# Rotary rows of a latent-attention encoder step: low parts taken before the halves are exchanged, rotations ended later in program order, key halves added on the vector engine

## The chip, the core and the metric

The kernel runs on one core of one Trainium2 chip. A core has a matrix engine (TensorE, PE in the profile; its weight loads are listed as PEld), a vector engine (VectorE, DVE), a scalar engine (ScalarE, ACT), a general engine (GpSimd, POOL) and an engine that here only issues DMAs (SyncE, SP; its queue is SPq in the profile). Each engine works through its own instructions in order and waits at one until what it needs is there. The metric is the device time of one execution in microseconds, as the median of several runs.

## What is computed

The program is one inference step of a one-layer encoder over 512 prompt frames and 32 frames of a running stream, 544 rows together: a layer norm, an input projection, eight heads of a gated linear recurrence, eight heads of latent attention, an output projection, and a gated feed-forward part. The change concerns the latent attention alone:

```python
q = (rms_norm(cq, q_a_g) @ w_q_b).reshape(B, T, MLA_HEADS, QK_NOPE + QK_ROPE)   # 128 + 64 per head
q_nope = q[..., :QK_NOPE]
q_rope = apply_rope(q[..., QK_NOPE:], cos[:, None, :], sin[:, None, :])
lat_new = rms_norm(ckv, kv_a_g)
kr_new = apply_rope(kr, cos, sin)
...
kv = (lat @ w_kv_b).reshape(B, past_len + T, MLA_HEADS, QK_NOPE + V_HEAD)
s = (jnp.einsum('bqhd,bkhd->bhqk', qn, k_nope)
     + jnp.einsum('bqhd,bkd->bhqk', qr, k_rope)).astype(jnp.float32) * scale

def apply_rope(x, cos, sin):
    x1, x2 = jnp.split(x, 2, axis=-1)
    return jnp.concatenate([x1 * cos - x2 * sin, x1 * sin + x2 * cos], axis=-1)
```

All results are float32.

## The kernel before

**Number format.** Most operands of matmuls are kept in the type `fp32r` (`R` in the code) in two parts, a high part (x rounded, by ACT) and a low part (x minus the high part, by DVE), and a product is the sum of high x high, high x low and low x high. `split_w` and `piece` do this for weights (L106 on ACT, L107 on DVE), `split_act` for activations (L176, L177), `mm3` issues the three products (L118).

**Layout.** Activations lie with features on the 128 partitions and the 544 rows along the free axis. Eight attention heads are worked on as four pairs. `proj_pair(pr)` computes for a pair the rotary query rows (`t == 2`, the 64 rotary features of both heads on 128 partitions), the plain query rows of each head (`t` 0 and 1), the plain keys `kn` of each head (L542, emptied by L546) and the values `vt` (L555, emptied by L558). `attend(pr)` computes scores (L585 plain, L587 rotary, mask at L588), the softmax, the transposes (L602, L603) and the value products (L616), in blocks of 128 queries; `scores` with `b == 4` is the running stream.

**Rotation.** `rope` exchanges the two halves of 32 features by four DMAs into `sw`, multiplies x by the cosines on POOL (in place, so after the DMAs have read x), `sw` by the sines on DVE, and adds the two on DVE into its targets. A rotary query tile `qr` of one head holds its 64 rounded rows on one half of the partitions and the low parts of these rows on the other, while the rotary key stands twice, `krs` rows 0 to 63 and again 64 to 127; one matmul thus takes both parts. To get the low part on the other half, `proj_pair` sends the rotated rows (`xr`) to the other partitions by two DMAs (`xo`, L525), rounds them there again on ACT (`xh`, L527) and subtracts on DVE (L530).

**Key rotation.** `kr_proj` multiplies by weights that hold their high parts in 64 columns and their low parts in the next 64, so that the two parts of the key come out on two halves of the partitions (L476). A matmul with a matrix `fold` of two identities adds them and puts the sum on both halves (L486). The outcome is rotated into `krs` and split into `krh` and `krl`.

**Memory.** The projections write PSUM tiles `main`, of which there are two; a third can only start once the first has been copied out (`hold`, on ACT). Temporaries of 128x544 come from the pool `t` with 7 buffers.

**Order.** The functions are generators. `weave` issues a few steps of a first list (projections) and then a step of a second (norms, attention). This gives the program order, and a scheduler of the language decides from it the order on every engine; within an engine nothing overtakes. All loads of weights and all DMAs of the rotation are issued by SP, in one queue.

Of the kernel before, what the change touches and what calls it, by code (L numbers as in the profile page):

```python
# [7 lines left out]
F32 = mybir.dt.float32  # L8
# [7 lines left out]
P = 128  # L16
D = 2048
KD = D // P
TP = 512
# [40 lines left out]
def tile_encoder_step(ctx, tc, xp, xs, w_in, w_in4, w_kr, w_q_b, w_kv_b, w_out, w_up, w_gate, w_down, w_down2,  # L60
# [31 lines left out]
    def main_tile():  # L92
        return psm.tile([P, 1024], F32, name="main", tag="main")
# [270 lines left out]
    with tc.tile_pool(name="mp", bufs=1) as mp, tc.tile_pool(name="psa", bufs=4, space=PSUM) as psa:  # L364
# [10 lines left out]
        krh = mp.tile([P, TP], R, name="krh")  # L375
# [10 lines left out]
        def tt():  # L386
            return mp.tile([P, T], F32, name="t", tag="t", bufs=7)
# [31 lines left out]
        def rope(x, dst_parts):  # L419
            sw = tt()  # L420
            for b in range(2):
                o = b * 64
                dma(sw[o:o + 32, :], x[o + 32:o + 64, :])
                dma(sw[o + 32:o + 64, :], x[o:o + 32, :])
            G.tensor_tensor(out=x, in0=x, in1=cos, op=ALU.mult)
            V.tensor_tensor(out=sw, in0=sw, in1=sin, op=ALU.mult)
            for dst, r, a, b in dst_parts:
                V.tensor_tensor(out=dst, in0=x[r, a:b], in1=sw[r, a:b], op=ALU.add)
# [37 lines left out]
        def kr_proj():  # L466
# [13 lines left out]
            fold, kp = tt()[:, :P], tt()  # L480
            for b in range(2):
                V.tensor_tensor(out=fold[:, 64 * b:64 * b + 64], in0=ident[:, :64], in1=ident[:, 64:], op=ALU.add)
            A.activation(kp, hold(kt), AF.Copy)
            kt = main_tile()
            for ps, j in both(kt):
                PE.matmul(ps, fold, kp[:, H_[j]], start=True, stop=True)  # L486
            kx = tt()
            A.activation(kx, hold(kt), AF.Copy)
            rope(kx, [(krs[:, :TP], slice(0, P), 0, TP), (krs[:, TP + PAST:], slice(0, P), TP, T)])
            dma(kr_d[:, :TP], krs[0:64, :TP])  # L490
            dma(kr_d[:, TP:], krs[0:64, TP + PAST:])
            krl = c["krl"] = hp.tile([P, T], R, name="krl", tag="hproj")[:, :TP]
            A.activation(krh, krs[:, :TP], AF.Copy)
            V.tensor_tensor(out=krl, in0=krs[:, :TP], in1=krh.bitcast(F32), op=ALU.subtract)
# [4 lines left out]
        def proj_pair(pr):  # L499
# [7 lines left out]
            qs = []  # L507
            for t in (2, 0, 1):
# [8 lines left out]
                if t == 2:  # L517
                    qr = ropes[pr % 2]
                    halves = list(enumerate((slice(0, 64), slice(64, P))))
                    xr, xo = tt(), tt()  # L520
                    rope(x, [(xr[:, :TP], slice(0, P), 0, TP)]
                         + [(qlast[pr % 2][r, 2, j * TS:(j + 1) * TS], r, TP, T) for j, r in halves])
                    xh = mp.tile([P, T], R, name="xh", tag="t", bufs=7)
                    for j, r in halves:
                        dma(xo[halves[1 - j][1], :TP], xr[r, :TP])  # L525
                        A.activation(qr[j][r], xr[r, :TP], AF.Copy)
                    A.activation(xh[:, :TP], xo[:, :TP], AF.Copy)  # L527
                    for j, r in halves:
                        o = halves[1 - j][1]
                        V.tensor_tensor(out=qr[j][o], in0=xo[o, :TP], in1=xh[o, :TP].bitcast(F32), op=ALU.subtract)  # L530
                    qs.append(qr)
                else:
                    G.tensor_copy(qlast[pr % 2][:, t, t * TS:(t + 1) * TS], x[:, TP:])
                    qs.append(x)
# [25 lines left out]
            pairs[pr] = qs[1:], qs[0], kn, vt  # L560
# [12 lines left out]
        def attend(pr):  # L573
# [3 lines left out]
            def scores(b, j):  # L577
# [8 lines left out]
                for i, k in enumerate((krh, c["krl"])):  # L586
                    PE.matmul(sc[:, :nk], qr[j][:, q0:q0 + P], k[:, :nk], start=False, stop=i == 1)  # L587
# [47 lines left out]
        weave([head_qf(0)], [ckv_norm()], 0.5)  # L635
# [1661 lines left out]
```

## Time and profile before

| | us |
|---|---|
| median of 3 runs | 2372.44 |
| lowest, highest | 2371.78, 2375.01 |
| the profiled execution | 2373.59 |
| its span, from the first to the last instruction | 2371.8 |
| TensorE busy in the span | 2320.4 |
| VectorE busy | 1801.2 |
| ScalarE busy | 1066.5 |
| GpSimd busy | 120.9 |
| mean granted clock of TensorE | 0.993 |

The span is what the views of the profile cover; the execution's own time has 1.8 us around it. A busy time is the sum of an engine's instructions; a matmul overlaps the next one, so the step from start to start, not the duration, says what one costs in a row. In a row of the timeline stand the start, the duration, engine, line, operation, the tile written and the tiles read, the shape, and how many equal instructions were merged; in brackets the idle time ahead and what ended it. The granted clock is the share of full speed at which TensorE ran.

The attention part with its projections lies between 70 and 310 us of the span. The input projection of the queries' norm comes before; the recurrence, the output projection and the feed-forward part come after.

### The profile page before, as it was taken

The numbers are of one execution on the slowest core, as the hardware profiler recorded it, in microseconds if no ns is written. First come the engines' busy times: TensorE is split into PE (matmuls) and PEld (weight loads), VectorE is DVE, ScalarE is ACT, GpSimd is POOL, SyncE is SP. The second block draws the span as 40 slices with busy tenths as digits, with TensorE's granted clock in tenths as the row PEclk, the third lists the DMA queues.
The fourth block names the chain that finished last, engine by engine and source line by source line (L and its number), as shares of the span: only waits on it lengthen the run. The fifth ranks groups of instructions, "written<-read, shape, count | busy, mean of one in ns | idle before, by whom it ended". The sixth has DMA issues, their size and how long they took to land.

```text
span 2371.8 us, 44419 instructions
## 1 busy us (share of the span) xinstructions
PE 2320.4 (98%) x18434; PEld 2303.8 (97%) x18434; DVE 1801.2 (76%) x2492; ACT 1066.5 (45%) x1659; POOL 120.9 (5%) x159
## 2 busy tenths in 40 slices
PE   7989999999999999999999999999999999999997
PEld 6989999999999999999999999999999999999997
DVE  7436668777786448989888888888777888888566
ACT  5335434433443226655555555555444433333334
POOL 1000000000001211000000000000000100000013
PEclk9999999999999999999999999999999999999998
DMA  7222263222235235544535435354343973643322
GB/s 243 90 87 71 75 205 99 87 85 86 91 133 199 90 107 198 164 165 144 194 113 165 149 121 192 105 178 135 112 131 118 363 295 115 238 139 96 108 73 76
DMA packets 128969, 334.25 MB, mean 141 GB/s; under 512 B 12032, under 2 KB 60928, under 8 KB 124160
## 3 DMA queue, kind: packets, MB, share of 16 engines
q1 hardware_dynamic: 121936, 285.73, 36.4%
q0 software_dynamic: 6832, 45.68, 4.9%
q8 instruction: 145, 2.38, 0.4%
q14 instruction: 56, 0.46, 0.1%
HBM read 272.78 MB, written 56.15 MB: 139 GB/s over the span
## 4 chain that ended last, share of the span: by engine, by line
PE 91%; DVE 4%; issue 2%; ACT 2%; DMA 1%; POOL 0%; SPq 0%; ACTq 0%; DVEq 0%; POOLq 0%
PE main L1248 21%; PE acc L1248 16%; PE main L118 14%; PE main L788 11%; PE main L1279 8%; PE acc L1279 6%; PE acc L118 6%; PE s L853 2%; PE main L555 1%; PE main L542 1%; PE at L616 1%; DVE wl L1194 1%; PE at L585 1%; PE sw L885 0%; PE sw L917 0%
## 5 line engine op out<-in xcount | busy, mean ns | idle before, releaser
L1193 ACT ACTIVATE wh<-raw 128x1024 fp32r<-128x1024 f32 x347 | 367.4, 1060 | 433.1 <-DVE raw L1186 132.7
L1194 DVE TENSOR_TENSOR wl<-raw,wh 128x1024 fp32r<-128x1024 f32 x347 | 424.3, 1223 | 131.2 <-ACT wh L1193 130.0
L1248 PE MATMUL main<-op,wh 128*128 128x272 f32 x1408 | 265.5, 287 | 0.0
L1248 PE MATMUL acc<-ops,wh 128*128 128x272 f32 x1344 | 254.2, 287 | 0.0
L1248 PE MATMUL main<-ops,wh 128*128 128x272 f32 x1344 | 254.2, 287 | 0.0
L1248 PEld LDWEIGHTS main<-op,wh 128*128 128x128 f32 x1408 | 221.0, 188 | 0.0
L1248 PEld LDWEIGHTS acc<-ops,wh 128*128 128x128 f32 x1344 | 211.0, 188 | 0.0
L1248 PEld LDWEIGHTS main<-ops,wh 128*128 128x128 f32 x1344 | 211.0, 188 | 0.0
L1248 PE MATMUL main<-op,wl 128*128 128x272 f32 x704 | 203.0, 288 | 0.3 <-DVE wl L1194 0.3
L1248 PE MATMUL acc<-ops,wl 128*128 128x272 f32 x672 | 193.7, 288 | 0.0
L1248 PE MATMUL main<-ops,wl 128*128 128x272 f32 x672 | 193.7, 288 | 0.0
L118 PE MATMUL main<-aH,wh 128*128 128x272 f32 (+2 forms) x736 | 176.8, 296 | 0.4 <-ACT wh L280 0.4
L118 PE MATMUL main<-aH,wl 128*128 128x272 f32 (+2 forms) x736 | 172.0, 290 | 3.0 <-DVE wl L281 3.0
L118 PE MATMUL main<-aL,wh 128*128 128x272 f32 (+2 forms) x736 | 171.9, 290 | 0.4 <-DVE aL L269 0.4
L1248 PE MATMUL acc<-op,wh 128*128 128x272 f32 x832 | 159.1, 289 | 3.5 <-DVE eg L1475 3.5
L107 DVE TENSOR_TENSOR wl<-raw,wh 128x1024 fp32r<-128x1024 f32 (+2 forms) x72 | 80.2, 1115 | 90.0 <-ACT wh L106 86.1
L1186 DVE TENSOR_TENSOR raw<-raw,raw 128x1024 f32<-128x1024 f32 x114 | 139.4, 1223 | 2.7
L732 ACT ACTIVATE wh<-raw 128x1024 fp32r<-128x1024 f32 x84 | 88.7, 1056 | 111.7 <-DVE raw L727 102.8
L1248 PEld LDWEIGHTS acc<-op,wh 128*128 128x128 f32 x832 | 131.7, 190 | 3.7 <-issue 3.7
L1248 PEld LDWEIGHTS main<-op,wl 128*128 128x128 f32 x704 | 132.3, 188 | 0.5 <-DVE wl L1194 0.5
L1194 DVE TENSOR_TENSOR wl<-rawl,wh 128x1024 fp32r<-128x1024 f32 x86 | 105.1, 1222 | 31.1 <-ACT wh L1193 31.1
L1193 ACT ACTIVATE wh<-rawl 128x1024 fp32r<-128x1024 f32 x86 | 91.0, 1059 | 82.3 <-DVE rawl L1186 42.4
(439 smaller groups left out, 6087.3 us busy)
## 6 DMA issues: line engine op xcount, KB each, us to landing
raw<-in_w_in SPq DMA_DIRECT2D x76, 512.0 KB, 3.6
raw<-in_w_up SPq DMA_DIRECT2D x72, 512.0 KB, 4.2
raw<-in_w_gate SPq DMA_DIRECT2D x72, 512.0 KB, 4.2
raw<-in_w_down SPq DMA_DIRECT2D x70, 512.0 KB, 4.0
raw<-in_w_out SPq DMA_DIRECT2D x40, 512.0 KB, 3.6
opd<-ohl SPq DMA_DIRECT2D x16, 1088.0 KB, 5.5
ops<-opd POOLq DMA_DIRECT2D x16, 1088.0 KB, 9.2
opd<-ohl SPq DMA_DIRECT2D x16, 816.0 KB, 6.2
```

The costliest lines, as they stand in the source:

```text
L107: V.tensor_tensor(out=dst(lv), in0=src(rv), in1=dst(hv).bitcast(F32), op=ALU.subtract)
L118: PE.matmul(ps, ww[:, wcols[0]:wcols[1]], aa[:, hs[j]], start=first and i == 0, stop=last and i == 2, skip_group_check=True)
L542: PE.matmul(ps[:, j * 512:j * 512 + 336], w[:, k, h * 256:h * 256 + 128], a[k][:, j * 336:(j + 1) * 336], start=k == 0 and i == 0, stop=k ...
L555: PE.matmul(ps[:, j * 512:j * 512 + 256], l[k][:, a:b], r4(w[:, k:k + 1, :])[:, 0, :, 128:256], start=k == 0 and i == 0, stop=k == 1 and i ...
L732: A.activation(wh, self.src, AF.Copy)
L788: PE.matmul(out, ww[:, k * P:(k + 1) * P], aa, start=name in ("11", "s1", "12") and k == 0 and q == 0, stop=k == HK - 1 and q == 2, skip_g ...
L853: PE.matmul(ps[:, j * 64:(j + 1) * 64], Kp[:, a:b], Qv[:, j * bt:(j + 1) * bt, 1, :], start=True, stop=True)
L1186: V.tensor_tensor(out=out, in0=a, in1=b, op=ALU.subtract)
L1193: A.activation(wh, src, AF.Copy)
L1194: V.tensor_tensor(out=wl, in0=src, in1=wh.bitcast(F32), op=ALU.subtract)
L1248: PE.matmul(ps, ww[:, k * P:(k + 1) * P], aa, start=self.first and k == 0 and i == 0, stop=k == n - 1 and i == 2, skip_group_check=True)
L1279: PE.matmul(banks[:, 512 * u:512 * u + NI], ww[:, (u * n + k) * P:(u * n + k + 1) * P], aa, start=self.first and k == 0 and i == 0, stop=k ...
```

## The change

The rotation of the queries is cut in two. The exchange of halves is issued right after the rotary rows (`t == 2`) are copied out; the rest of the rotation stands in the program after the copy of the first plain rows (`t == 0`). The low parts are now subtracted where the rows lie (`low`, L533) and two DMAs carry them straight into the other half of the query tiles (L534). The second rounding (`xh`), the exchanged copy (`xo`) and the separate target (`xr`) are gone; the last columns are copied by POOL.

For the key, the two halves are exchanged by two DMAs and added on DVE (L487) in place of the matmul with `fold`. This and the rotation move to a function `kr_rope`, which is woven into the first projection of the recurrence behind the norm of the latents. `krh` moves to another pool, and `t` has 8 buffers.

```diff
         def tt():
-            return mp.tile([P, T], F32, name="t", tag="t", bufs=7)
+            return mp.tile([P, T], F32, name="t", tag="t", bufs=8)
...
-        def rope(x, dst_parts):
+        def swapped(x, n):
             sw = tt()
-            for b in range(2):
-                o = b * 64
-                dma(sw[o:o + 32, :], x[o + 32:o + 64, :])
-                dma(sw[o + 32:o + 64, :], x[o:o + 32, :])
+            for o in range(0, P, 2 * n):
+                dma(sw[o:o + n, :], x[o + n:o + 2 * n, :])
+                dma(sw[o + n:o + 2 * n, :], x[o:o + n, :])
+            return sw
+
+        def rope(x, sw, dst_parts):
             G.tensor_tensor(out=x, in0=x, in1=cos, op=ALU.mult)
             V.tensor_tensor(out=sw, in0=sw, in1=sin, op=ALU.mult)
...
-            fold, kp = tt()[:, :P], tt()
-            for b in range(2):
-                V.tensor_tensor(out=fold[:, 64 * b:64 * b + 64], in0=ident[:, :64], in1=ident[:, 64:], op=ALU.add)
+            kp = tt()
             A.activation(kp, hold(kt), AF.Copy)
-            kt = main_tile()
-            for ps, j in both(kt):
-                PE.matmul(ps, fold, kp[:, H_[j]], start=True, stop=True)
-            kx = tt()
-            A.activation(kx, hold(kt), AF.Copy)
-            rope(kx, [(krs[:, :TP], slice(0, P), 0, TP), (krs[:, TP + PAST:], slice(0, P), TP, T)])
+            c["kp"] = kp, swapped(kp, 64)
+
+        def kr_rope():
+            kx, other = c["kp"]
+            V.tensor_tensor(out=kx, in0=kx, in1=other, op=ALU.add)
+            sw = swapped(kx, 32)
+            yield
+            yield
+            rope(kx, sw, [(krs[:, :TP], slice(0, P), 0, TP), (krs[:, TP + PAST:], slice(0, P), TP, T)])
...
                 x = tt()
                 A.activation(x, hold(ps), AF.Copy)
                 if t == 2:
-                    qr = ropes[pr % 2]
-                    halves = list(enumerate((slice(0, 64), slice(64, P))))
-                    xr, xo = tt(), tt()
-                    rope(x, [(xr[:, :TP], slice(0, P), 0, TP)]
-                         + [(qlast[pr % 2][r, 2, j * TS:(j + 1) * TS], r, TP, T) for j, r in halves])
-                    xh = mp.tile([P, T], R, name="xh", tag="t", bufs=7)
+                    qx, sw = x, swapped(x, 32)
+                    continue
+                G.tensor_copy(qlast[pr % 2][:, t, t * TS:(t + 1) * TS], x[:, TP:])
+                qs.append(x)
+                if t == 0:
+                    rope(qx, sw, [(qx, slice(0, P), 0, T)])
+                    low = mp.tile([P, T], R, name="low", tag="t", bufs=8)
                     for j, r in halves:
-                        dma(xo[halves[1 - j][1], :TP], xr[r, :TP])
-                        A.activation(qr[j][r], xr[r, :TP], AF.Copy)
-                    A.activation(xh[:, :TP], xo[:, :TP], AF.Copy)
+                        A.activation(qr[j][r], qx[r, :TP], AF.Copy)
+                        G.tensor_copy(qlast[pr % 2][r, 2, j * TS:(j + 1) * TS], qx[r, TP:])
                     for j, r in halves:
-                        o = halves[1 - j][1]
-                        V.tensor_tensor(out=qr[j][o], in0=xo[o, :TP], in1=xh[o, :TP].bitcast(F32), op=ALU.subtract)
-                    qs.append(qr)
-                else:
-                    G.tensor_copy(qlast[pr % 2][:, t, t * TS:(t + 1) * TS], x[:, TP:])
-                    qs.append(x)
+                        V.tensor_tensor(out=low[r, :TP], in0=qx[r, :TP], in1=qr[j][r].bitcast(F32), op=ALU.subtract)
+                        dma(qr[j][halves[1 - j][1]].bitcast(F32), low[r, :TP].bitcast(F32))
...
-        weave([head_qf(0)], [ckv_norm()], 0.5)
+        weave([head_qf(0)], [ckv_norm(), kr_rope()], 0.5)
```

The places at which the order on the engines changes, with line numbers of each kernel's own code (the changed one counts up to four lines differently here: L516 is L520 after, L428 is L429, L526 is L530, L406 is L405, L415 is L414):

On TensorE at the end of the key projection, before (`at` is a small PSUM tile; the last two rows are the first of the recurrence's projection):

```order
L476 MATMUL main<-aH,wh 128x272 x2
L476 MATMUL main<-aL,wh 128x272 x2
L406 MATMUL at<-ones,t 128x1 x5
L415 MATMUL at<-ident,r_1365 128x128
L486 MATMUL main<-t 128x272 x2
L118 MATMUL main<-aH,wh 128x272 x2
L118 MATMUL main<-aL,wh 128x272 x2
```

And after, twelve rows of that projection further on, around the same sums (L405):

```order
L118 MATMUL main<-aL,wh 128x272 x2
L118 MATMUL main<-aH,wl 128x272 x2
L405 MATMUL at<-ones,t 128x1 x5
L118 MATMUL main<-aH,wh 128x272 x2
L118 MATMUL main<-aL,wh 128x272 x2
L118 MATMUL main<-aH,wl 128x272 x2
```

The sums of the latents' norm moved from the end of the key projection into the next projection, the broadcasts (L414) another 24 rows behind them, and L486 is gone.

On ACT in pair 0, before (L516 copies query rows out of PSUM, first the rotary ones, then t=0 and t=1; L546 copies plain keys):

```order
L516 ACTIVATE t_1627<-main_1602 128x544
L106 ACTIVATE wh_1794<-raw_1792 128x2x256
L106 ACTIVATE wh_1794<-raw_1792 128x2x128
L106 ACTIVATE wh_2008<-raw_2006 128x1024
L526 ACTIVATE qr00_937<-t_1629 64x512
L526 ACTIVATE qr01_938<-t_1629 64x512
L527 ACTIVATE xh_1641<-t_1630 128x512
L516 ACTIVATE t_1674<-main_1649 128x544
L516 ACTIVATE t_1702<-main_1677 128x544
L546 ACTIVATE kn_1724<-main_1711 128x672
L546 ACTIVATE kn_1739<-main_1726 128x672
```

And after:

```order
L520 ACTIVATE t_1623<-main_1598 128x544
L520 ACTIVATE t_1655<-main_1630 128x544
L106 ACTIVATE wh_1787<-raw_1785 128x2x256
L106 ACTIVATE wh_1787<-raw_1785 128x2x128
L106 ACTIVATE wh_1998<-raw_1996 128x1024
L546 ACTIVATE kn_1717<-main_1704 128x672
L530 ACTIVATE qr00_937<-t_1623 64x512
L530 ACTIVATE qr01_938<-t_1623 64x512
L520 ACTIVATE t_1695<-main_1670 128x544
L546 ACTIVATE kn_1732<-main_1719 128x672
```

The copy of t=0 moved ahead of the weight splits, the copy of t=1 and the roundings behind the first keys, and L527 is gone.

On DVE in pair 0, before (`t_1631` is the exchanged copy times the sines):

```order
L107 TENSOR_TENSOR wl_1795<-raw_1792,wh_1794 128x2x256
L107 TENSOR_TENSOR wl_1795<-raw_1792,wh_1794 128x2x128
L426 TENSOR_TENSOR t_1631<-t_1631,sin_929 128x544
L107 TENSOR_TENSOR wl_2009<-raw_2006,wh_2008 128x1024
L428 TENSOR_TENSOR t_1629<-t_1627,t_1631 128x512
L428 TENSOR_TENSOR ql0_942<-t_1627,t_1631 64x32 x2
L530 TENSOR_TENSOR qr00_937<-t_1630,xh_1641 64x512
L530 TENSOR_TENSOR qr01_938<-t_1630,xh_1641 64x512
```

And after:

```order
L107 TENSOR_TENSOR wl_1788<-raw_1785,wh_1787 128x2x256
L107 TENSOR_TENSOR wl_1788<-raw_1785,wh_1787 128x2x128
L427 TENSOR_TENSOR t_1625<-t_1625,sin_929 128x544
L107 TENSOR_TENSOR wl_1999<-raw_1996,wh_1998 128x1024
L429 TENSOR_TENSOR t_1623<-t_1623,t_1625 128x544
L533 TENSOR_TENSOR low_1661<-t_1623,qr00_937 64x512
L533 TENSOR_TENSOR low_1661<-t_1623,qr01_938 64x512
```

The place of the sum (L428, now L429) among the weight splits is the same; the low parts (L533) follow it as L530 did, but write `low` and not the query tiles.

More of the change, by code (lines that the diff above doesn't have):

```diff
@@ L374, in tile_encoder_step @@
         ropes = [[mp.tile([P, TP], R, name=f"qr{g}{j}", tag=f"qr{g}{j}") for j in range(2)] for g in range(2)]
-        krh = mp.tile([P, TP], R, name="krh")
         qlast = [mp.tile([P, 3, P], F32, name=f"ql{g}", tag=f"ql{g}") for g in range(2)]
@@ L479, in kr_proj @@
                         yield
-            fold, kp = tt()[:, :P], tt()
-            for b in range(2):
-                V.tensor_tensor(out=fold[:, 64 * b:64 * b + 64], in0=ident[:, :64], in1=ident[:, 64:], op=ALU.add)
+            kp = tt()
             A.activation(kp, hold(kt), AF.Copy)
-            kt = main_tile()
-            for ps, j in both(kt):
-                PE.matmul(ps, fold, kp[:, H_[j]], start=True, stop=True)
-            kx = tt()
-            A.activation(kx, hold(kt), AF.Copy)
-            rope(kx, [(krs[:, :TP], slice(0, P), 0, TP), (krs[:, TP + PAST:], slice(0, P), TP, T)])
+            c["kp"] = kp, swapped(kp, 64)
[6 more added lines that the diff above has]
+            rope(kx, sw, [(krs[:, :TP], slice(0, P), 0, TP), (krs[:, TP + PAST:], slice(0, P), TP, T)])
+            krh, krl = c["kr"] = [hp.tile([P, T], R, name=n, tag="hproj")[:, :TP] for n in ("krh", "krl")]
+            A.activation(krh, krs[:, :TP], AF.Copy)
+            V.tensor_tensor(out=krl, in0=krs[:, :TP], in1=krh.bitcast(F32), op=ALU.subtract)
             dma(kr_d[:, :TP], krs[0:64, :TP])
             dma(kr_d[:, TP:], krs[0:64, TP + PAST:])
-            krl = c["krl"] = hp.tile([P, T], R, name="krl", tag="hproj")[:, :TP]
-            A.activation(krh, krs[:, :TP], AF.Copy)
-            V.tensor_tensor(out=krl, in0=krs[:, :TP], in1=krh.bitcast(F32), op=ALU.subtract)
         VT = [(0, 128), (128, 256), (256, 384), (384, 512), (512, 640), (544, 672)]
@@ L507, in proj_pair @@
             qs = []
+            qr = ropes[pr % 2]
+            halves = list(enumerate((slice(0, 64), slice(64, P))))
             for t in (2, 0, 1):
@@ L559, in proj_pair @@
                              ps.rearrange("p (j c) -> p j c", j=2)[:, :, :256], AF.Copy)
-            pairs[pr] = qs[1:], qs[0], kn, vt
+            pairs[pr] = qs, qr, kn, vt
         def softmax(sc, nq, keys):
@@ L585, in scores @@
                 PE.matmul(sc[:, :nk], qn[j][:, q0:q0 + P], kn[j][:, :nk], start=True, stop=False)
-                for i, k in enumerate((krh, c["krl"])):
+                for i, k in enumerate(c["kr"]):
                     PE.matmul(sc[:, :nk], qr[j][:, q0:q0 + P], k[:, :nk], start=False, stop=i == 1)
```

## The prediction

> **What bounds the kernel now.** I read the page first, then the list of what TensorE waits for, then a table of stages, and last the instructions in order of time around the two places that the list names.
>
> ```profile
> span 2371.8 us, 44419 instructions
> PE 2320.4 (98%) x18434; PEld 2303.8 (97%) x18434; DVE 1801.2 (76%) x2492; ACT 1066.5 (45%) x1659; POOL 120.9 (5%) x159
> ```
> TensorE (PE) is busy for 98% of the span, so the only time to be had is in the 51.4 us in which it is idle, in matmuls that go, and in matmuls that run at a lowered clock. Next, TensorE's waits, longest in total first (engine, line waited at, releaser: total us, times, longest):
>
> ```profile
> PE main L542 <- ACT t L516: 9.9, 3, 9.5
> PE at L415 <- POOL r L410: 1.5, 1, 1.5
> ```
> Both lie in the code of the diff. L542 is the key projection of a head pair, held up by the emptying of PSUM on ScalarE (ACT) at L516; 9.5 of its 9.9 us are one wait, in pair 0. L415 is the norm of the key-value latents, held up by GpSimd's (POOL's) power. The table by stage (us, busy time of PE, PEld, DVE, ACT and POOL with counts, then the granted clock) shows what follows such a gap:
>
> ```profile
> 112.00:116.00 4.00, 2.49 (x23) 2.41 (x21) 1.08 (x2) 1.57 (x2) 1.17 (x1) 0.95 0.36 105
> 116.00:120.00 4.00, 4.00 (x17) 3.53 (x18) 0.31 (x1) 0.62 (x1) 0.00 (x0) 0.63 0.00 0
> 152.80:162.30 9.50, 0.04 (x1) 0.05 (x1) 4.27 (x8) 3.31 (x6) 0.15 (x1) 0.70 0.46 125
> 162.30:166.30 4.00, 4.00 (x14) 4.00 (x15) 0.80 (x2) 0.69 (x2) 0.63 (x2) 0.50 0.00 0
> 900.00:1850.00 950.00, 945.46 (x7530) 944.47 (x7529) 811.22 (x873) 513.28 (x794) 10.67 (x14) 1.00 0.45 153
> ```
> After the gap of 1.5 us the granted clock is 0.63, after that of 9.5 us it is 0.50 for 4 us: each gap is paid twice. The last row stands for the rest of the program: TensorE is busy for 945.46 of 950 us, so what comes before only shifts it, and a microsecond saved early is saved at the end.
>
> **Part 1, the key rotation's own projection (kr_proj, L473 to L494).** Removed from TensorE are the two fp32 matmuls of L486; the latents' norm no longer stands right behind the key projection. Before, 5 small matmuls (L406) are followed at once by L415, which must wait for DVE and POOL. After, the sums (now L405) stand behind 12 rows of the first recurrence projection, and the broadcasts (now L414, L415) 24 rows further on.
>
> ```profile
> 83.63 1.25 PE L406 MATMUL at<-ones,t 128*128 128x1 f32 x10 [0.20 <-issue]
> 84.74 0.50 PE L118 MATMUL main<-aL,wh 128*128 128x272 f32 x2
> 89.08 1.05 PE L415 MATMUL at<-ident,r 128*128 128x128 f32 x8
> 90.11 0.50 PE L118 MATMUL main<-aH,wh 128*128 128x272 f32 x2
> 113.28 1.17 PE L406 MATMUL at<-ones,t 128*128 128x1 f32 x10
> 115.96 0.80 PE L415 MATMUL at<-ident,r 128*128 128x128 f32 x2 [1.51 <-POOL r L410]
> 116.54 2.02 PE L486 MATMUL main<-t 128*128 128x272 f32 x4
> 119.15 0.42 PE L118 MATMUL main<-aH,wl 128*128 128x272 f32 x2
> 127.68 0.83 PE L415 MATMUL at<-ident,r 128*128 128x128 f32 x6
> 128.48 0.50 PE L118 MATMUL main<-aH,wh 128*128 128x272 f32 x2
> ```
> From 113.28 to 119.15, 5.87 us pass; the rest of the broadcasts takes 128.48 - 127.68 = 0.80. In these 6.67 us TensorE does the sums, the broadcasts, L486 and four matmuls of L118. The same norm for the queries, with other matmuls around it and no gap, shows the price without waits: sums 84.74 - 83.63 = 1.11, broadcasts 90.11 - 89.08 = 1.03, and four matmuls of L118, two rows, 0.50 (34 such rows stand between 119.15 and 127.68, 0.25 each). That is 2.64, so this part saves 4.0 us. The cover for the POOL wait is now 24 matmul rows, about 6 us (24 x 0.25), against a wait of 1.5; without it the 1.5 and the slow clock would stay. The halves are added on DVE instead (one more 128x544 sum, 0.7 us) after two more DMAs on SP, then come four DMAs, the rotation and the latents' norm. DVE is busy for 0.31 of 4 us here, and the first reader of the rotated keys (L587) is at 173.99, some 50 us later: I cost them at nothing. DVE's sin product now stands ahead of the latents' norm and may hold it for the DMAs; the latents are wanted at 152.8.
>
> **Part 2, the query rotation of pair 0 (L516 to L530).** The chain of the long gap, from the timelines of ACT, DVE and SP's queue and the chain of waits:
>
> ```profile
> 132.24 0.69 DVE L107 TENSOR_TENSOR wl<-raw,wh 128x512 fp32r<-128x512 f32 x1 [1.10 <-ACT wh L106]
> 147.51 0.56 SPq L423 DMA_DIRECT2D t<-t  x1
> 151.78 1.72 DVE L107 TENSOR_TENSOR wl<-raw,wh 128x512 fp32r<-128x512 f32 x1 [4.67 <-ACT wh L106]
> 155.53 0.68 DVE L428 TENSOR_TENSOR t<-t 128x512 f32<-128x512 f32 x1
> 156.24 1.27 ACT L526 ACTIVATE qr<-t 64x512 fp32r<-64x512 f32 x2 [2.62 <-DVE t L428]
> 156.23 1.15 SPq L525 DMA_DIRECT2D t<-t  x2
> 156.80 4.03 DMA t<-t
> 161.06 0.63 ACT L527 ACTIVATE xh<-t 128x512 fp32r<-128x512 f32 x1 [3.56 <-DMA t<-t]
> 161.60 1.12 ACT L516 ACTIVATE t<-main 128x544 f32<-128x544 f32 x2
> 162.26 0.93 PE L542 MATMUL main<-latH,wh 128*128 128x336 f32 x2 [9.49 <-ACT t L516]
> 168.09 0.28 PE L555 MATMUL main<-wh,latH 128*128 128x256 f32 x1
> 189.49 0.47 PE L542 MATMUL main<-latL,wh 128*128 128x336 f32 x2
> 190.71 0.47 PE L542 MATMUL main<-latH,wl 128*128 128x336 f32 x2
> ```
> TensorE ends its query projections at T = 162.26 - 9.49 = 152.77. Both L516 copies (t=0 and t=1) stand on ACT behind L527, which waits for the exchange by DMA, 4.03 us; PSUM has two main tiles, so both key projections wait. They then run slow: 5.83 us to L555, though 24 of them take 3.66 at full clock (12 rows of (190.71 - 189.49) / 4 = 0.305). From T to L555 pass 15.32 us.
>
> After, L527 is gone, the t=0 copy stands ahead of the weight splits, and the first key projection uses its buffer: it starts at T and ends at T + 2.0 (1.83 and some fill). The t=1 copy stands behind the two roundings (L530), which wait for DVE's sum (L429). What is ahead of that sum on DVE is as before, so I leave it at 155.53: with 544 columns, 0.71, it ends at T + 3.5. Roundings 1.27, copy 0.55 (half of the row of two), wake 0.05: the second key projection starts at T + 5.35. A gap of 3.35 us remains. It is likely to leave TensorE slow again. The 9.5 us gap cost 5.83 - 3.66 = 2.2 us of pace; the 1.5 us gap cost 119.15 - 115.96 = 3.19 less what this work takes at full clock (0.26 for L415, a quarter of 1.03; an estimate of 0.9 for L486 from the same rows by columns; 0.50), some 1.5. I take 1.9 between them. L555 then starts at T + 5.35 + 1.83 + 1.9 = T + 9.1, and the part saves 6.2 us. Its ends: 11.7 (no gap, no slow clock: 15.32 - 3.66) and nothing (the sum 6 us later than I have it).
>
> The Trainium skill speaks against the size of this last loss: "TensorE: Matmul & The Clock Gate", What's actually happening, has the clock halved only after an idle window of about 3.4 us, in a window that runs freely. By it the gap that is left might cost no pace at all, and the sum would be 1.9 better. The 0.63 behind the 1.5 us gap speaks for a shorter idle time, though matmuls of one column lie just ahead of it.
>
> The low parts are now computed in place (L533, two at half of 1.4, like L530 before) and sent by two DMAs straight into the query tiles, where L587 reads them. The roundings end at T + 4.8, DVE at about T + 5.6, SP's two issues (1.15) at T + 6.8; with the longest landing here, 4.03, they are there by T + 10.8.
>
> ```profile
> 173.99 0.30 PE L587 MATMUL at<-krh,qr 128*128 128x128 f32 x1
> ```
> Before, L587 came 173.99 - 168.09 = 5.9 us behind L555; now that is T + 15.0. The cover is 4 us, made of the 36 value matmuls and the first 12 of the next pair. GpSimd's extra copies of last columns have no reader before scores 4.
>
> **Part 3, pairs 1 to 3.** There TensorE has attention work to put in the gap, and little is left to gain. Pairs 2 and 3 show it, under the step at full pace from pair 1:
>
> ```profile
> 187.64 0.79 PE L587 MATMUL at<-krh,qr 128*128 128x512 f32 x1
> 188.27 0.40 PE L587 MATMUL at<-krl,qr 128*128 128x512 f32 x1
> 220.87 0.80 PE L587 MATMUL at<-krh,qr 128*128 128x512 f32 x1
> 221.93 0.57 PE L542 MATMUL main<-latH,wh 128*128 128x336 f32 x2 [0.26 <-ACT t L516]
> 254.39 0.80 PE L587 MATMUL at<-krh,qr 128*128 128x512 f32 x1
> 255.35 0.57 PE L542 MATMUL main<-latH,wh 128*128 128x336 f32 x2 [0.17 <-ACT t L516]
> ```
> The next matmul came 0.63 after L587 in pair 1, 1.06 in pair 2 and 0.96 in pair 3: 0.43 and 0.33 lost. With the t=0 copy ahead these go: 0.8. The second key projection stands behind another set of scores, some 3 us after the first starts, and the t=1 copy is due about when the first starts: hidden. One ACT pass of 0.63 per pair goes too, on an engine that is not the bound. The low parts are wanted a whole attention later.
>
> **The sum.** 4.0 + 6.2 + 0.8 = 11.0 us. The profiled execution took 2373.59; that gives 2362.6. The median, 2372.44, stands 1.15 lower: 2361.4.
>
> **Rivals.**
> - *The gap in pair 0 closes.* If DVE's sum is ready before TensorE ends the first key projection (3.35 us sooner than I have it), the part saves 11.7, all 16.5: 2355.9. For it: DVE's 128x512 split ahead of it took 1.72 us, against 0.69 at 132.24, so a microsecond might go by itself. Against it: the 128x1024 split ahead of the sum stays. 0.12.
> - *The clock holds through the remaining gap.* Everything as forecast without the 1.9 us: 2359.5. For it: the gap is a third of the 9.5; against it: the 0.63 after 1.5 us. This is the time by the page's rule too. 0.11.
> - *The wait only changes its releaser.* The t=1 copy is held as long as both were, because sum and roundings still stand ahead of it and the exchange lands some 6 us later (SP's queue now has two more DMAs ahead, at the keys). Then 4.0 + 0.8 remain: 2367.6, about the border of no change. For it: the copy does stand behind an exchange by DMA; against it: that one is issued at 147.51, 5 us ahead of T. 0.10.
> - *Slower: the low parts come late to L587.* They are no longer finished by an engine but by a DMA, the last step of the chain, and SP issues in order behind two weight loads that wait for free buffers. Past 4 us of delay each microsecond costs TensorE one, and it would take 4 + 11 + 5 = 20 us late in pair 0 to be slower by 0.2%, five times the longest landing here. 0.03.
>
> **How the numbers follow.** The forecast, 2361.4, has 0.64; its own range is 2358.5 to 2364.5 (part 1 from 3 to 4.5, part 2 from 4.5 to 7.5, part 3 from 0 to 1.5, ends seldom together). The range for all, 2356 to 2366, leaves out the third and fourth rival and a little of the first, under 0.2. A measurement of this kernel can tell about 0.2%, 4.7 us, from no change. Faster by more: 0.64 + 0.12 + 0.11 = 0.87; within: 0.10; slower: 0.03.
>
> **What would show it.** Right: no wait of TensorE at the latents' broadcast and a clock of 1.00 from 108 to 148; in pair 0 a first key projection that follows the query projections at once, then a gap of 3 to 4 us released by the t=1 copy on ACT; no wait at L587. Part 1 is wrong if a gap stands at L414 or the head's evacuations wait for the latents; part 2 if the gap is below 1 us or above 6; the whole if TensorE waits for a DMA of the low parts, or if a stage behind 310 us gets longer.

## The result, and the profile after

| | before | after |
|---|---|---|
| median, us (4 runs each, one chip) | 2373.44 | 2358.39 |
| lowest, highest | 2371.78, 2375.01 | 2357.42, 2358.93 |
| profiled execution | 2373.59 | 2358.93 |
| its span | 2371.8 | 2357.2 |

The ratio is 0.9936, with an interval of 0.9919 to 0.9953: the change makes the kernel faster by about 15 us. The forecast was 2361.4, from a median before of 2372.44; that was the median of three of these runs, and the fourth raises it to 2373.44. The time lies within the range of 2356 to 2366, a tenth of a microsecond below the likeliest case's own range (2358.5 to 2364.5), between the two rivals in which the rest of pair 0's gap costs less (2355.9 and 2359.5), and nearer to the second of them than to the forecast. By the medians the gain is 15.05 us against the 11.0 of the prediction's sum; the time came out only 3.0 below the forecast because the starting median was 1.0 too low. So the direction and the places were right, and two of the three terms were too small.

The page after, first the span, then the engines:

```profile
span 2357.2 us, 44395 instructions
PE 2317.3 (98%) x18430; PEld 2302.0 (98%) x18430; DVE 1798.8 (76%) x2483; ACT 1064.4 (45%) x1654; POOL 121.9 (5%) x167
```
The span is 14.6 us shorter and TensorE's busy time 3.1, so 11.5 of the 14.6 us gained were idle time of TensorE. What TensorE waits for between 140 and 165 us, after:

```profile
PE main L542 <- ACT kn L546: 0.8, 1, 0.8
PE main L555 <- ACT t L520: 0.6, 1, 0.6
```
In place of the wait of 9.5 stand two, of 0.8 and 0.6, and the first of them has another releaser than I had forecast. The table by stage, after (columns as in the prediction's; after the five engines come the granted clock, the DMA share and GB/s), in the four stretches where before had its gaps or where after has what is left of them:

```profile
112.00:116.00 4.00, 4.00 (x34) 4.00 (x34) 0.73 (x2) 1.57 (x2) 0.00 (x0) 1.00 0.28 104
116.00:120.00 4.00, 4.00 (x36) 4.00 (x35) 1.92 (x3) 0.00 (x0) 1.45 (x1) 1.00 0.71 191
148.00:152.00 4.00, 3.42 (x25) 3.13 (x23) 3.44 (x4) 2.44 (x4) 1.58 (x1) 1.00 0.10 24
152.00:156.00 4.00, 3.16 (x20) 2.97 (x21) 2.54 (x4) 2.69 (x5) 0.63 (x3) 1.00 0.75 230
```
At the key projection's end TensorE is now busy for all of 8 us at a clock of 1.00, with 70 matmuls in place of 40. In pair 0 the clock stays at 1.00 through both small gaps.

To see where the time went, I cut the span at five instructions that every kernel of this study has: the copy out of PSUM at the end of the key projection (key), the copy of pair 0's rotary rows (rot), the first value projection of pair 0 (val), the first copy of the recurrence (rec), and the end. These rows, from ACT's and TensorE's timelines, before:

```profile
113.48 0.62 ACT L483 ACTIVATE t<-main 128x544 f32<-128x544 f32 x1 [2.92 <-PE main L476]
146.80 0.62 ACT L516 ACTIVATE t<-main 128x544 f32<-128x544 f32 x1 [0.33 <-PE main L118]
308.19 0.62 ACT L357 ACTIVATE hproj<-main 128x544 f32<-128x544 f32 x1 [1.93 <-PE main L118]
```
and after (before, val is the row of L555 at 168.09 in the prediction):

```profile
114.28 0.62 ACT L482 ACTIVATE t<-main 128x544 f32<-128x544 f32 x1 [2.92 <-PE main L477]
143.59 0.63 ACT L520 ACTIVATE t<-main 128x544 f32<-128x544 f32 x1 [0.34 <-PE main L118]
155.18 0.39 PE L555 MATMUL main<-wh,latH 128*128 128x256 f32 x1 [0.61 <-ACT t L520]
293.70 0.62 ACT L357 ACTIVATE hproj<-main 128x544 f32<-128x544 f32 x1 [1.93 <-PE main L118]
```

| stretch, us | before | after | saved | forecast |
|---|---|---|---|---|
| start to key | 113.48 | 114.28 | -0.8 | 0 |
| key to rot (part 1) | 33.32 | 29.31 | 4.0 | 4.0 |
| rot to val (part 2) | 21.29 | 11.59 | 9.7 | 6.2 |
| val to rec (part 3) | 140.10 | 138.52 | 1.6 | 0.8 |
| rec to end | 2063.6 | 2063.5 | 0.1 | 0 |
| sum | 2371.8 | 2357.2 | 14.6 | 11.0 |

The first row is not the change's: this copy began between 113.1 and 114.5 in all 14 profiles, and the two executions of the changed kernel had 114.28 and 113.16.

### The profile page after: what moved, and what is told of

Read it like the earlier page. It is cut to its first block, busy times and chain, and to the rows that moved or that the text cites. A ratio compares the mean times of both kernels' runs of the same rounds, so it can differ in the third digit from the quotient of the medians.

```text
span 2357.2 us, 44395 instructions
## 1 busy us (share of the span) xinstructions
PE 2317.3 (98%) x18430; PEld 2302.0 (98%) x18430; DVE 1798.8 (76%) x2483; ACT 1064.4 (45%) x1654; POOL 121.9 (5%) x167
## 4 chain that ended last, share of the span: by engine, by line
PE 93%; DVE 3%; DMA 1%; ACT 1%; issue 1%; POOL 0%; ACTq 0%; SPq 0%; DVEq 0%
PE main L1248 21%; PE acc L1248 16%; PE main L118 16%; PE main L788 11%; PE main L1279 8%; PE acc L1279 6%; PE acc L118 6%; PE s L853 2%; PE main L555 1%; PE at L616 1%; PE at L585 1%; DMA x<-in_xp 1%; DVE wl L1194 1%; PE main L542 0%; DMA raw<-in_w_in 0%
```

## The experiments

My theory after the result: the key part and the query part act each by itself; in the query part it is the place of the rotation's end that counts, and the prediction mis-sized it because the PSUM tiles are not taken by turns. In the built program both plain key tiles of pair 0 lie in one and the same PSUM bank, and the first value tile takes the one that the t=1 copy frees; so the second keys wait only for the copy of the first. The traces agree: the second keys start at 152.24, while the t=1 rows are in their tile until 155.13 (the rows stand in the section on the prediction). The rivals: most of the gain is that the exchange by DMA is gone from the chain; or the gap's size doesn't depend on the tiles and only the clock was luckier. The table has every kernel's stretches by the same five instructions, from the profile, and the median of its timed runs (for "one" a single run was made). The runs were made on several chips, so each ratio below, and each gain in a median, is against runs of before on the same chip: 2373.96 for the first four experiments, 2373.16 for the next four, 2373.00 for the repeats.

| kernel | median, us | key to rot | rot to val | rot to rec | rec to end |
|---|---|---|---|---|---|
| before | 2373.44 | 33.32 | 21.29 | 161.39 | 2063.6 |
| after | 2358.39 | 29.31 | 11.59 | 150.11 | 2063.5 |
| key part alone | 2370.02 | 29.31 | 20.53 | 161.02 | 2062.0 |
| query part alone | 2360.18 | 31.86 | 11.51 | 150.17 | 2063.5 |
| fold kept | 2360.60 | 33.47 | 11.39 | 149.96 | 2061.6 |
| rotation ended at t=2 | 2364.44 | 29.31 | 17.62 | 156.55 | 2063.0 |
| exchange kept | 2359.24 | 29.31 | 11.65 | 151.99 | 2063.3 |
| rotation ended at t=1 | 2356.26 | 29.31 | 9.50 | 148.99 | 2062.0 |
| turns kept | 2361.00 | 29.31 | 15.11 | 154.35 | 2062.6 |
| four more hops | 2361.33 | 29.31 | 11.70 | 153.32 | 2063.1 |
| before, again | 2375.03, one | 34.74 | 20.49 | 160.60 | 2063.5 |
| query part alone, again | 2363.01, one | 33.32 | 11.46 | 150.12 | 2064.6 |
| after, again | 2357.90 | 29.31 | 11.59 | 150.20 | 2063.1 |
| t=1, again | 2356.76 | 29.31 | 9.50 | 149.01 | 2064.2 |

**The key part alone.** The changed key code, with the query rotation as before:

```diff
-                    qx, sw = x, swapped(x, 32)
-                    continue
...
-                if t == 0:
-                    rope(qx, sw, [(qx, slice(0, P), 0, T)])
...
+                    xr, xo = tt(), tt()
+                    rope(x, swapped(x, 32), [(xr[:, :TP], slice(0, P), 0, TP)]
...
+                    A.activation(xh[:, :TP], xo[:, :TP], AF.Copy)
```

> The key part alone (halves added on DVE, key rotation moved), queries as before. My account: the traces of before and after give this part 4.0 us (milestones: rotary rows of pair 0 copied out at 146.80 and 143.59, less the 0.80 by which the key projection itself ended later), and the long wait in pair 0 stays at 9.5 us with a clock of 0.5 behind it: about 2369.4 against 2373.4. Rival: the two parts help each other, and this one alone gives less than 2 us because the wait in pair 0 grows: above 2371.5.

2370.02, 0.9984 of before (0.9976 to 0.9993), 3.9 us less, and the long wait stands where it was, as its list of waits shows:

```profile
PE main L544 <- ACT t L518: 9.4, 1, 9.4
```
The first part is worth what its sum gave (2369.4 was expected), and it does nothing for the second: from rot to rec this run takes 161.02, the two of before 161.39 and 160.60.

**The query part alone.** The changed query code; fold matmul and key rotation as before:

```diff
-            c["kp"] = kp, swapped(kp, 64)
...
+            kt = main_tile()
+            for ps, j in both(kt):
+                PE.matmul(ps, fold, kp[:, H_[j]], start=True, stop=True)
...
-        weave([head_qf(0)], [ckv_norm(), kr_rope()], 0.5)
+        weave([head_qf(0)], [ckv_norm()], 0.5)
```

> The query part alone (low parts before the exchange, rotation ended after t = 0), keys as before. My account: 9.7 us in pair 0 and 1.6 in pairs 1 to 3, 2362.1; the second plain keys of pair 0 use the PSUM tile of the first and wait for its copy (0.8 us), not for the copy of t = 1. The gap of 1.5 us at the latents' broadcast stays, with a clock near 0.6 behind it. Rival: as the prediction had it, a gap of 3.35 us and a slow clock: 2366.

2360.18, 0.9943 (0.9929 to 0.9957): 13.8 us less than before, where 11.3 were expected. From rot to rec it takes 150.17 against after's 150.11, so the query part does not need the key part. But its key to rot is 31.86, not 33.32. The gap of 1.5 us is there again, but the clock behind it stays at 1.00, where about 0.6 was expected:

```profile
112.00:116.00 4.00, 2.49 (x22) 2.41 (x21) 1.22 (x2) 1.57 (x2) 1.17 (x1) 1.00 0.31 100
116.00:120.00 4.00, 4.00 (x30) 3.84 (x31) 0.17 (x1) 0.63 (x1) 0.00 (x0) 1.00 0.12 29
```
Part 1's gain is thus a short wait and two matmuls, which always go, and a slow stretch that can only go where it had come. The repeats below take that up.

**The rotation ended at t=2.** All as after, but the sum, the roundings and the low parts stand in the program where the old code had them, right behind the exchange:

```diff
                 if t == 2:
                     qx, sw = x, swapped(x, 32)
-                    continue
-                G.tensor_copy(qlast[pr % 2][:, t, t * TS:(t + 1) * TS], x[:, TP:])
-                qs.append(x)
-                if t == 0:
+                else:
+                    G.tensor_copy(qlast[pr % 2][:, t, t * TS:(t + 1) * TS], x[:, TP:])
+                    qs.append(x)
+                if t == 2:
```

> The changed kernel, but the rotation ends right after the rotary rows (t = 2) in the program, as before; the low parts stay as changed. It tells the later place from the dropped exchange and second rounding. Theory that the place does most: both copies of t = 0 and t = 1 stand behind the two roundings, TensorE waits from the end of the query projections for about 5.4 us (DVE's sum 3.5, roundings 1.27, copy 0.6) and then runs slow: 5 us more than the changed kernel, 2363.5. Theory that the dropped exchange does most: within 1.5 us of the changed kernel, below 2360.

2364.44, 0.9959 (0.9945 to 0.9972), near the 2363.5 expected if the place does most. From rot to rec 6.4 us of the 11.3 gained are lost again. The key projection waits 5.58 us (5.4 expected), and the table shows the slow clock behind:

```profile
154.35 0.93 PE L542 MATMUL main<-latH,wh 128*128 128x336 f32 x2 [5.58 <-ACT t L520]
152.00:156.00 4.00, 1.65 (x6) 1.65 (x7) 1.71 (x3) 2.39 (x4) 0.83 (x4) 0.57 0.80 225
156.00:160.00 4.00, 4.00 (x18) 4.00 (x17) 0.00 (x0) 0.73 (x1) 0.00 (x0) 0.58 0.05 12
```
The place of the rotation's end does more than half. What stays, 4.8 us, is the exchange and second rounding that are gone from ACT's queue.

**The exchange kept.** The opposite half: the old exchange, second rounding and low parts, but ended at t=0:

```diff
                 if t == 0:
-                    rope(qx, sw, [(qx, slice(0, P), 0, T)])
...
+                    xr, xo = tt(), tt()
+                    rope(qx, sw, [(xr[:, :TP], slice(0, P), 0, TP)]
...
+                        dma(xo[halves[1 - j][1], :TP], xr[r, :TP])
+                        A.activation(qr[j][r], xr[r, :TP], AF.Copy)
+                    A.activation(xh[:, :TP], xo[:, :TP], AF.Copy)
```

> The changed kernel, but with the low parts as before (rotated rows exchanged, rounded a second time, subtracted); the rotation ends after t = 0 as changed. Theory that the place does most: the copy of t = 1 stands behind the second rounding, but only the last value matmuls need its PSUM tile: 1 to 2 us more than the changed kernel, 2359.4 to 2360.4. Theory that the dropped exchange does most: 5 us or more lost, above 2363.

2359.24, 0.9939 (0.9925 to 0.9952), near the 2359.4 to 2360.4 expected if the place does most. As expected, only the last value matmuls wait for the t=1 copy; from the list of waits between 140 and 300 us:

```profile
PE main L558 <- ACT t L520: 0.4, 1, 0.4
```
From rot to rec it loses only 1.9 of the 11.3. Taken singly, a later place gains 9.4 (161.39 - 151.99) and dropping the exchange 4.8 (161.39 - 156.55), or 8.6 and 4.0 from the second execution of before (160.60): they overlap, since each shortens the same wait. The rival "the exchange does most" falls.

**The fold kept.** As after, but with the fold matmul in place of the sum on DVE:

```diff
-            c["kp"] = kp, swapped(kp, 64)
+            kt = main_tile()
+            for ps, j in both(kt):
+                PE.matmul(ps, fold, kp[:, H_[j]], start=True, stop=True)
+            kx = tt()
+            A.activation(kx, hold(kt), AF.Copy)
+            c["kx"] = kx, swapped(kx, 32)
```

> The changed kernel, but the key's halves are again added by the matmul with fold, in a second PSUM tile; the key rotation stays in its new place. In the built order the latents' sums and the first broadcast are back right behind the key projection. Theory that the matmul's PSUM tile holds up the next projection and that the rest of the 4.0 us follows from it: the gap of 1.5 us and the slow clock return whole, 2362.4. Theory that the moved rotation does it: under 1.5 us lost, about 2359.5 (the two matmuls' own 0.9).

2360.60, 0.9947 (0.9934 to 0.9961). In the trace all of part 1 is gone: key to rot takes 33.47. Sums and first broadcast stand right behind the key projection again, and its list of waits and its table have the row of before:

```profile
PE at L414 <- POOL r L409: 1.5, 1, 1.5
116.00:120.00 4.00, 4.00 (x18) 3.62 (x18) 0.11 (x1) 0.62 (x1) 0.00 (x0) 0.57 0.07 16
```
So the later key rotation alone does not let the next projection begin ahead of the norm; the fold matmul has to go. Whether its PSUM tile holds that projection up, or the matmul's place in the order, is not shown, and neither is whether the matmul's going would do without the later rotation. The time, taken alone, would have misled: it lies between the two expected (2362.4 and 2359.5), nearer to the second. The profiled executions of this kernel and of after are only 1.1 us apart (2360.02 and 2358.93), because here the start is 1.0 shorter and the tail 1.9, both outside the stretch of the edit (the last section shows one thing that shortened the tail).

**The turns kept.** To test the step that failed, I made the main PSUM tiles alternate by force, in the whole program, and kept the scheduler from reordering TensorE's work in pair 0:

```diff
-        return psm.tile([P, 1024], F32, name="main", tag="main")
+        turn_of[0] += 1
+        return psm.tile([P, 1024], F32, name="main", tag=f"main{turn_of[0] % 2}", bufs=1)
...
-        run(proj_pair(0))
+        with tc.manual_schedule(engines={mybir.EngineType.PE}):
+            run(proj_pair(0))
```

> The changed kernel with what the prediction assumed: PSUM tiles strictly by turns, and TensorE's order in pair 0 as in the program, so that the second plain keys wait for the copy of t = 1. By the prediction's step: a gap of 3.4 to 3.9 us ahead of them, then a slow clock that costs 1.5 to 2.2, values begin 3 to 4 us later than in the changed kernel: 2361.4 to 2362.5. Rival by the rule on the clock (an idle window of about 3.4 us that runs freely): the gap alone, no slow clock, 2360.3.

2361.00, 0.9949 (0.9933 to 0.9964). By the time alone this lies between the two expected (2361.4 to 2362.5 with a slow clock, 2360.3 without); the trace decides. Ahead of the second keys TensorE now waits twice, 0.82 and 2.45 us with two matmuls of scores between, together 3.27 where the prediction had 3.35, and the clock falls. The rows are from TensorE's timeline and from the table:

```profile
151.45 0.49 PE L588 MATMUL at<-kn,t 128*128 128x128 f32 x2 [0.82 <-ACT kn L549]
154.40 0.93 PE L545 MATMUL main<-latH,wh 128*128 128x336 f32 x2 [2.45 <-ACT t L523]
152.00:156.00 4.00, 1.60 (x6) 1.61 (x7) 1.75 (x3) 1.88 (x3) 0.62 (x3) 0.60 0.68 182
156.00:160.00 4.00, 4.00 (x19) 4.00 (x19) 0.00 (x0) 0.73 (x1) 0.00 (x0) 0.54 0.07 15
```
From rot to val it takes 15.11. The prediction's account for that order comes to 14.9: T + 9.1, with T 5.82 behind rot (149.41 - 143.59). The step was priced rightly for a program that is not the one built. The run changes two things at once; that it is the tile that holds the second keys follows from their wait, which ends with the t=1 copy.

**Four more hops.** To see whether the low parts can be late at the rotary scores, four more DMAs in a chain carry them:

```diff
+                    hop1, hop2 = tt(), tt()
...
-                        dma(qr[j][halves[1 - j][1]].bitcast(F32), low[r, :TP].bitcast(F32))
+                        o = halves[1 - j][1]
+                        dma(hop1[o, :TP], low[r, :TP].bitcast(F32))
+                        dma(hop2[r, :TP], hop1[o, :TP])
+                        dma(hop1[o, :TP], hop2[r, :TP])
+                        dma(hop2[r, :TP], hop1[o, :TP])
+                        dma(qr[j][o].bitcast(F32), hop2[r, :TP])
```

> The changed kernel, but each low part makes four more hops by DMA before it reaches the query tile, some 11 to 12 us later (2.2 to landing and 0.6 of issue each). It tests the prediction's slower rival, that past a cover of about 4 us each microsecond of delay costs TensorE one. By that: a wait of about 7 us at the first rotary scores of pair 0 and a slow clock behind it, 2367. Rival: the scheduler puts other matmuls ahead of these scores (the built order has them some 36 matmuls later), and most is hidden: 2359 to 2361.

2361.33, 0.9951 (0.9938 to 0.9965). No wait at the rotary scores (L593 here): the program's order had put them later, behind matmuls of the next projection. Of the 3.2 us more from rot to rec, 1.7 are idle time of TensorE in small waits elsewhere (3.15 us idle, against 1.43 after); the rest lies in the steps of the matmuls, which I did not take apart. First the rotary scores' row, then the longest in the list of waits from 150 to 300 us, of which the first two are near those of after, and last a row of ACT's timeline:

```profile
166.42 0.23 PE L593 MATMUL at<-krh,qr 128*128 128x128 f32 x1
PE main L548 <- ACT kn L552: 0.8, 1, 0.8
PE main L561 <- ACT kn L552: 0.7, 1, 0.7
PE main L561 <- ACT vt L564: 0.7, 1, 0.7
166.42 0.63 ACT L520 ACTIVATE t<-main 128x544 f32<-128x544 f32 x1 [2.87 <-DMA t<-t]
```
The hops also take two of the eight buffers of `t` and more of SP's queue, and a later copy of query rows on ACT waited 2.87 us for a DMA. I had expected 2367 from a wait at those scores; the rival account, that there is none, was nearer. The slower rival's mechanism didn't appear even here, but because the order moves with the delay, and because of those buffers, this run doesn't say at which delay it would begin.

**The rotation ended at t=1.** If a later place helps, one later still may help more:

```diff
-                if t == 0:
+                if t == 1:
                     rope(qx, sw, [(qx, slice(0, P), 0, T)])
```

> The changed kernel, but the rotation ends after the copy of t = 1, one projection later. In the built order that copy stands ahead of the first plain keys' copy, and the PSUM tiles go by turns again. Theory: both short waits of the changed kernel in pair 0 (0.82 and 0.61) shrink to one of 0.7 for the second keys' copy behind the roundings: 0.7 us faster than the changed kernel, 2357.7. Rival: the roundings come later and the low parts land too late for the first rotary scores: 1 us or more slower, 2359.5.

2356.26, 0.9930 (0.9917 to 0.9942). The t=1 copy now stands ahead of the roundings, and one wait is left:

```profile
150.26 0.60 ACT L520 ACTIVATE t<-main 128x544 f32<-128x544 f32 x1
153.09 1.28 ACT L530 ACTIVATE qr<-t 64x512 fp32r<-64x512 f32 x2 [1.02 <-DVE t L429]
154.40 0.73 ACT L546 ACTIVATE kn<-main 128x672 f32<-128x672 f32 x1
155.18 0.39 PE L555 MATMUL main<-wh,latH 128*128 128x256 f32 x1 [0.63 <-ACT kn L546]
```
From rot to rec it takes 148.99, 1.1 us less than after, where 0.7 was expected. Here the PSUM tiles go by turns, and it costs nothing, since the second keys' tile was emptied (150.26 + 0.60) before they start (151.14).

**Four repeats, one chip.** Before, the query part alone, after and the version ended at t=1, each unchanged.

> The kernel before once more, for a second profile. In its first the gap of 1.5 us at the latents' broadcast was followed by a clock of 0.63 (17 matmuls in 4 us), in the run of the query part alone, with the same code there, by 1.00 (30 matmuls). Theory that the slow clock after a short gap comes and goes from one execution to the next: either of the two here, and a change as well in the 400 us from 908 to 1308 of the span (3139 matmuls, or 3152), where seven runs showed both. Rival: it is a trait of each program: 0.63 again, 3139 again.

> The query part alone once more, for a second profile. Theory that the slow clock after the 1.5 us gap comes and goes: either, 1.00 or near 0.6; from the end of the key projection to the copy of the rotary rows then 31.9 us or 33.4. Rival: a trait of the program: 31.9 again.

> The changed kernel once more, on one chip with the next. Theory: 2358.4 again, and from the copy of pair 0's rotary rows to the first gate copy of the recurrence 150.1 us in the trace, whatever start and end of the program do.

> The version whose rotation ends after t = 1 once more, on one chip with the changed kernel. Theory: the same stretch is 149.0 us again, 1.1 less than in the changed kernel, and the time 1 to 2 us less. Rival: the 2 us between their medians came from where start and end happened to fall, and the stretches are equal.

After came to 2357.90 (0.9934, 0.9922 to 0.9947) and the version ended at t=1 to 2356.76 (0.9928, 0.9915 to 0.9942); from rot to rec they take 150.20 and 149.01, within 0.1 of what they took the first time. So 1.1 to 1.2 us between the two are there in both pairs of traces, and the medians of both pairs have the same sign; the single timed runs overlap a little. It is the best version here. The query part alone, the same program as above, took 33.32 from key to rot this time, with the slow clock behind the same gap:

```profile
112.00:116.00 4.00, 2.49 (x21) 2.41 (x20) 1.38 (x2) 1.57 (x2) 1.17 (x1) 0.91 0.37 101
116.00:120.00 4.00, 4.00 (x19) 3.53 (x19) 0.01 (x1) 0.62 (x1) 0.00 (x0) 0.66 0.00 0
```
30 matmuls stood there in the first execution, 19 in this one. Before, again, had only 9 in that stretch (its gap began later), a clock of 0.54, and 34.74 from key to rot.

## Why the prediction was right or wrong

**Part 1, right.** The norm's sums left the end of the key projection, no wait is left at the broadcast, and the clock is 1.00 from 112 to 120; 4.0 us were forecast, 4.0 are in the trace, 3.9 in the run of this part alone. All nine profiles without the fold matmul take 29.31 from key to rot. The five with it took 31.86 to 34.74, depending on the clock behind the gap: the gain in an execution is 2.6 to 5.4 us, and 4.0 is the value of the compared pair. That the forecast met it to a tenth is in part luck. DVE's sum, the extra DMAs and the later key rotation cost nothing that the traces show.

**Part 2, right in place and direction, wrong in one step: 9.7 for 6.2.** The first key projection does follow the query projections at once. The step that failed is "A gap of 3.35 us remains": it rests on the second key projection's start behind the t=1 copy, and the kernel had other PSUM tiles there. By the prediction's own sign (a gap below 1 us) part 2 was wrong. TensorE's timeline after:

```profile
149.41 0.47 PE L542 MATMUL main<-latH,wh 128*128 128x336 f32 x2
152.24 0.58 PE L542 MATMUL main<-latH,wh 128*128 128x336 f32 x2 [0.82 <-ACT kn L546]
154.19 0.38 PE L585 MATMUL at<-kn,t 128*128 128x128 f32 x2
```
From T = 149.41, the first keys take 2.01, the wait for the first keys' own copy 0.82, the second keys 1.95, two matmuls of scores and the wait for the t=1 copy together 0.99: L555 is at T + 5.77, not T + 9.1. Of the 3.3 between, 1.9 is the gap (3.35 less 0.82 and 0.61) and 1.9 the slow clock that didn't come, less some 0.5 for the second keys' pace and the scores. The t=1 copy's own time was forecast within half a microsecond; it only was wanted later, by the values, behind the second keys. ACT's timeline:

```profile
151.45 0.73 ACT L546 ACTIVATE kn<-main 128x672 f32<-128x672 f32 x1 [0.98 <-PE main L542]
153.20 1.29 ACT L530 ACTIVATE qr<-t 64x512 fp32r<-64x512 f32 x2 [1.01 <-DVE t L429]
154.51 0.62 ACT L520 ACTIVATE t<-main 128x544 f32<-128x544 f32 x1
```
It ends at T + 5.72 (154.51 + 0.62), where I had T + 5.3. That the clock's loss in the forecast was real for the larger gap, the kernel with turns kept shows (0.60 and 0.54, with 3.27 us of idle time). The rival by which the clock holds comes nearest in time (2359.5), but by luck: the clock held because the gap was smaller. The Trainium skill ("TensorE: Matmul & The Clock Gate", What's actually happening) halves the clock after an idle window of about 3.4 us. In the kernel with turns kept, idle times of 0.82 and 2.45 us with half a microsecond of matmuls between were enough.

**The low parts, right.** Low parts issued as forecast, on SP's queue, and the rotary scores that read them:

```profile
154.57 1.23 SPq L534 DMA_DIRECT2D qr<-low  x2
161.06 0.22 PE L587 MATMUL at<-krh,qr 128*128 128x128 f32 x1
```
L587 comes 5.88 behind L555 as before, and nothing waits there. The issues end at 155.80, and these two took 2.2 to 2.3 us from issue to landing: some 3 us of cover are left, against 4.0 forecast. It shrank because L555 came earlier, by more than the landing was shorter than the 4.03 I had taken.

**Part 3, right in sign, twice the size.** 1.6 us against 0.8. By the copies of the plain keys, which move 13.46 us earlier in pair 1, 13.91 in pair 2 and 14.52 in pair 3, it is spread evenly, about half a microsecond from each pair to the next; I had costed pair 1 at nothing. From val to rec TensorE was idle for 0.5 us before and not at all after; the other 1.1 lie in the steps of the matmuls, and which of them I did not take apart.

**The sum.** The three terms are 4.3 short (15.3 against 11.0); start and tail, which the change does not touch, take 0.7 back, which leaves 14.6 in the profiles. By the medians of the first comparison the difference was larger, 15.05, within their spread.

## What to carry to other kernels

An instruction that empties PSUM should not stand in its engine's queue behind work that waits for something far away: moving the end of a rotation behind the next copies gained more (8.6 to 9.4 us) than taking the DMA out of its chain (4.0 to 4.8 us). Before a wait for a PSUM tile is priced, see which bank each tile got in the built program: with turns forced, and TensorE's order in pair 0 held, nearly the same code was 4.2 us slower from rot to rec, while in the fastest version here, ended at t=1, the tiles go by turns. And where a few microseconds decide, compare stretches between the same instructions in the traces, since a median carries one or two microseconds of clock that belong to no edit.

## What the runs showed of the hardware that I had not expected

The slow clock behind a gap comes and goes between executions of one program. Behind the 1.5 us gap at the norm the granted clock was lowered in four of five profiles that have it (0.54 to 0.66 over the 4 us that hold most of it) and at 1.00 in one, of the same program as one of the four. Far behind all edits, near 1000 us, every kernel has another gap of 3.5 us, in which TensorE waits for DVE. The 4 us behind it in the two executions of the version ended at t=1 (us, TensorE's busy time, granted clock, DMA share, GB/s):

```profile
998.14:1002.14 4.00, 4.00 (x32) 1.00 0.53 216
998.32:1002.32 4.00, 4.00 (x18) 0.50 0.75 304
```
In 11 of the 14 profiles the clock there was 0.50 to 0.68, in three it was 1.00; and these three (the key part alone, the fold kept, the version ended at t=1) have the three shortest tails of the table from rec to end, 2061.6 to 2062.0, against 2062.6 to 2064.6. So part of the tail's scatter goes with this one gap: at the slowest, 18 matmuls stand in those 4 us and not 32, and at the 0.125 us of one at full clock that is 1.75 us, of a scatter of 3.0. The Trainium skill, on the page and in the section named above, has the activity window run freely and an idle window of about 3.4 us halve the clock; that a gap of 3.5 us does so in some executions and not in others agrees with that. The share does not: if the whole window must be idle, a gap of 3.5 us holds one for only some 3% of its positions (an estimate from that figure of the Trainium skill: 0.1 / 3.4), and here the clock fell in 11 of 14. The 1.5 us gap doesn't fit the figure either: even with the one-column matmuls just ahead of it counted as idle, it is 2.7 us long (113.28 to 115.96, before). The 2.45 comes near it, with the 0.82 half a microsecond ahead: 3.27 us idle within 3.77. Gaps of 0.82 and 0.61 us left the clock at 1.00 where I looked (after, the exchange kept, ended at t=1). From which length on a gap puts the clock at risk isn't settled by these runs.
